# Hymba-style layer on one core: values and gates in 512 columns, two groups' MLP down by Strassen–Winograd with weight sums kept in scratch

## The chip, the cores and the metric

The kernel runs on one core of a Trainium2 chip. The metric is the device time of one execution in microseconds (us). Engines are named as in the profile: PE (TensorE) with its weight loads PEld, DVE (VectorE), ACT (ScalarE), POOL (GpSimd), SP (SyncE, which here only issues DMAs); POOL and ACT also issue DMAs.

## What is computed

One layer for 2,048 prompt tokens and 128 sample tokens (8 streams of 16) of width 1,024, all in float32: an HGRN2 recurrence and a banded attention side by side, the output projection, and a squared-ReLU MLP of width 4,096. Cut to what the change touches:

```python
h = rmsnorm(x, norm1_g)
proj = h @ w_in                      # 1024 -> 4 x 512 (hq, hf, hi, hg) + 3 x 512 (aq, ak, av)
hq, hf, hi, hg, aq, ak, av = jnp.split(proj, SPLITS, axis=-1)
o_h, s_new = hgrn2_scan(hq, 1 - fgate, hi, log(fgate), s0)   # hi: the values
o_h = rmsnorm(o_h, hg_norm_g) * silu(hg)                     # hg: the gates
...
x = x + concat([o_h, o_a]) @ w_out
u = rmsnorm(x, norm2_g) @ w_up                               # 1024 -> 4096
x = x + square(relu(u)) @ w_down                             # 4096 -> 1024
y = rmsnorm(x, final_norm_g)
```

## The kernel before, in words

**Products.** Tokens lie in 17 tiles of 128 (tile 16 is the sample). A float32 operand is held as two arrays, hi (rounded to fp32r, by ACT) and lo (the rest, by DVE). Each product of a pair is three matmuls into one PSUM tile, hi·hi, hi·lo and lo·hi (`mm3`, L337 to L339). Matmuls are written here as 128x256, 128x384 and so on, by the columns that stream.

**Weights.** `W` (L294) loads 128x1024 raw values with one DMA of 512 KB on SP's queue and splits them in two pieces of 128x512 (L303 on ACT, L304 on DVE). A weight of 1024x256 is four pieces. The generator `wseq` hands the weights out in the order of use and makes one ahead; the pool `wsp` holds eight pieces.

**Order.** The program is written as Python generators that `weave` interleaves by cost numbers; a list scheduler then fixes each engine's instruction order. On the chip every engine runs its own list strictly in order and waits on semaphores, so a waiting instruction holds up everything behind it on its engine.

**Stages.** `phase_hgrn` (about 0 to 650 us) projects tokens in six groups of two or three tiles (`hgrn_proj`) while the recurrence of the group before runs. The values (column blocks 4 and 5 of `w_in`) and the gates (blocks 6 and 7) are made with tokens on the PSUM partitions, by `tok`, 256 columns at a time: 24 matmuls of 128x256 per tile and block, then an eviction (ACT for values; ACT, POOL L435 and DVE for gates). `phase_att` runs to about 1380 us. `phase_mlp` then runs three groups of 6, 6 and 5 tiles. The transposed normalised input of a group is two SBUF arrays, `h_hi` and `h_lo`. In the course of group 0 `side` also does the sample's attention and output projection (`sample_mixer`), and makes `h` of group 1 (`prepare`, with `transpose_split` and its L117); that of group 2 is made beside group 1.

**One step of the MLP.** A group takes 16 steps (`fc`), each for 256 of the 4,096 hidden columns. Up: four chunks of 24 matmuls 128x384 (128x320 in the group of 5), each followed by ReLU on ACT (L1138), square on DVE (L1139) and the split into `uh` and `ul` (L1141, L1142). Down: for each tile and each 512 output columns, six matmuls 128x512 into one of four PSUM tiles and an add into `y` on DVE (L1161). The next steps' weights are loaded and split beside it. After the last step each tile is normalised and written out.

## Time and profile before

| What | Value |
|---|---|
| Three timed runs | 2984.89, 2985.36 and 2981.88 us, median 2984.89 us |
| The profiled execution, its own time | 2982.84 us |
| Its span in the trace | 2980.8 us |
| Busy share | PE 97%, DVE 59%, ACT 38%, POOL 10% |
| DMA | 328.17 MB, 110 GB/s over the span |
| Granted clock of PE, mean | 0.99 of full speed (2.4 GHz) |

The profile is of one execution. Its time is 2.05 us below the median of the three runs and 2.04 us above its span. Busy shares are means over stages; the windows among the rows below give them by stage. The three-array form of every product shows as three lines, L337, L338 and L339, of equal counts. The times to landing of DMAs count from the issue.

### The profile page before, as it was taken

To read this page: it belongs to the slowest core of one execution; us is meant where nothing else is said; L and a number is where in the kernel's file an instruction comes from. 1 tells how busy PE (TensorE), PEld (TensorE's weight loads), DVE (VectorE), ACT (ScalarE), POOL (GpSimd) and SP (SyncE) were. 2 spreads that over 40 slices of the span, in tenths; PEclk is the share of its full clock that TensorE was granted. 3 is DMA by queue.
4 is the path that set the end of the run, shared out by engine and by line. 5 is a ranking of instruction groups with operands and counts; after the bars stand their busy time and mean duration, and the time that the engine had idled before them with its cause. 6 is when DMAs were issued, how large, how long until landed. Compare 5 with 4: busy or idle time off the path is not lost.

```text
span 2980.8 us, 47227 instructions
## 1 busy us (share of the span) xinstructions
PE 2899.4 (97%) x18967; PEld 2674.6 (90%) x18967; DVE 1748.5 (59%) x3127; ACT 1117.9 (38%) x2290; POOL 292.5 (10%) x491
## 2 busy tenths in 40 slices
PE   8999999989999999998999999999999999999997
PEld 7989999989888899998888999999999999899997
DVE  6665665765556565665556455565555555555554
ACT  5523433435545455553223223232222223323222
POOL 3311231221010101011000000010000000000000
PEclk9999999999999999999999999999999999999999
DMA  8443423434333434447322322242212123222221
GB/s 275 156 126 100 127 94 95 141 103 139 107 119 106 132 105 137 145 155 268 114 85 89 115 85 91 64 156 64 78 57 71 57 69 126 83 78 71 83 73 64
DMA packets 113125, 328.17 MB, mean 110 GB/s; under 512 B 12613, under 2 KB 36937, under 8 KB 112906
## 3 DMA queue, kind: packets, MB, share of 16 engines
q1 hardware_dynamic: 104570, 299.20, 31.7%
q0 software_dynamic: 6320, 18.62, 1.6%
q10 hardware_dynamic: 2016, 7.34, 0.8%
q8 instruction: 148, 2.42, 0.3%
q14 instruction: 71, 0.58, 0.1%
HBM read 292.61 MB, written 32.51 MB: 109 GB/s over the span
## 4 chain that ended last, share of the span: by engine, by line
PE 71%; DVE 2%; ACT 2%; DMA 1%; issue 1%; POOL 0%; SPq 0%; ACTq 0%; POOLq 0%; DVEq 0%
PE mm L337 21%; PE mm L339 21%; PE mm L338 21%; PE ps_oT L788 3%; PE S L781 2%; PE S L759 2%; PE tx L114 1%; DMA x<-x 1%; ACT junk L100 1%; ACT s L772 0%; PE ps_os L850 0%; DVE y L124 0%; DVE wlo L304 0%; POOL r L92 0%; ACT whi L303 0%
## 5 line engine op out<-in xcount | busy, mean ns | idle before, releaser
L303 ACT CAST whi<-wraw 128x512 fp32r<-128x512 f32 x816 | 498.7, 620 | 723.5 <-PE mm L339 555.1
L304 DVE TENSOR_TENSOR wlo<-wraw,whi 128x512 fp32r<-128x512 f32 x816 | 572.4, 717 | 224.0 <-ACT whi L303 215.9
L337 PE MATMUL mm<-h_hi,whi 128*128 128x384 f32 (+1 forms) x1536 | 504.4, 328 | 3.4 <-DVE h_lo L117 3.4
L339 PE MATMUL mm<-h_hi,wlo 128*128 128x384 f32 (+1 forms) x1536 | 502.7, 327 | 0.0
L338 PE MATMUL mm<-h_lo,whi 128*128 128x384 f32 (+1 forms) x1536 | 501.9, 327 | 0.0
L1161 DVE TENSOR_TENSOR y<-mm,y 128x512 f32<-128x512 f32 x544 | 373.3, 689 | 219.0 <-PE mm L339 217.2
L339 PE MATMUL mm<-whi,ul 128*128 128x512 f32 x1088 | 424.3, 390 | 0.3 <-DVE ul L1142 0.2
L338 PE MATMUL mm<-wlo,uh 128*128 128x512 f32 x1088 | 424.0, 390 | 0.0
L337 PE MATMUL mm<-whi,uh 128*128 128x512 f32 x1088 | 423.5, 389 | 0.5 <-ACT uh L1141 0.5
L337 PE MATMUL mm<-whi,hT_hi 128*128 128x256 f32 x1264 | 376.7, 298 | 21.1 <-ACT whi L303 7.9
L339 PE MATMUL mm<-whi,hT_lo 128*128 128x256 f32 x1264 | 367.6, 291 | 3.1 <-DVE hT_lo L206 1.8
L338 PE MATMUL mm<-wlo,hT_hi 128*128 128x256 f32 x1264 | 364.3, 288 | 0.3 <-DVE wlo L304 0.3
L337 PEld LDWEIGHTS mm<-h_hi,whi 128*128 128x128 f32 x1536 | 289.4, 188 | 8.3 <-DVE h_lo L117 3.6
L338 PEld LDWEIGHTS mm<-h_lo,whi 128*128 128x128 f32 x1536 | 289.4, 188 | 1.2
L339 PEld LDWEIGHTS mm<-h_hi,wlo 128*128 128x128 f32 x1536 | 289.2, 188 | 0.0
L337 PEld LDWEIGHTS mm<-whi,hT_hi 128*128 128x128 f32 x1264 | 245.0, 194 | 33.9 <-ACT whi L303 8.6
L1139 DVE SCALAR_TENSOR_TENSOR u<-mm,u 128x384 f32<-128x384 f32 (+1 forms) x192 | 102.4, 533 | 281.8 <-ACT u L1138 281.8
L337 PE MATMUL mm<-hT_hi,whi 128*128 128x384 f32 (+1 forms) x768 | 260.3, 339 | 4.1 <-ACT qs L965 4.0
L339 PE MATMUL mm<-hT_hi,wlo 128*128 128x384 f32 (+1 forms) x768 | 253.2, 330 | 1.0 <-DVE wlo L304 1.0
L338 PE MATMUL mm<-hT_lo,whi 128*128 128x384 f32 (+1 forms) x768 | 253.4, 330 | 0.0
L339 PEld LDWEIGHTS mm<-whi,hT_lo 128*128 128x128 f32 x1264 | 245.3, 194 | 8.8 <-issue 3.6
L338 PEld LDWEIGHTS mm<-wlo,hT_hi 128*128 128x128 f32 x1264 | 245.6, 194 | 2.0 <-issue 1.0
(200 smaller groups left out, 4024.8 us busy)
## 6 DMA issues: line engine op xcount, KB each, us to landing
wraw<-in_w_in SPq DMA_DIRECT2D x168, 512.0 KB, 4.1
wraw<-in_w_up SPq DMA_DIRECT2D x96, 512.0 KB, 3.9
wraw<-in_w_down SPq DMA_DIRECT2D x96, 512.0 KB, 4.0
wraw<-in_w_out SPq DMA_DIRECT2D x48, 512.0 KB, 3.9
xT<-in_x_T SPq DMA_DIRECT2D x34, 512.0 KB, 3.9
og<-og SPq DMA_DIRECT2D x17, 512.0 KB, 3.8
x<-yo POOLq DMA_DIRECT2D x68, 128.0 KB, 3.3
x<-x SPq DMA_DIRECT2D x17, 512.0 KB, 5.0
```

The source lines that it names most:

```text
L100: nc.scalar.activation(junk[:, :n], x, AF.Square, accum_out=ss)
L114: nc.tensor.transpose(ps[:, k, :], src[:, (k0 + k) * P:(k0 + k + 1) * P], c.ident)
L303: nc.scalar.copy(hi, rw)
L304: nc.vector.tensor_tensor(out=lo, in0=rw, in1=hi.bitcast(F32), op=ALU.subtract)
L337: nc.tensor.matmul(ps, lh, rh, start=(i == 0), stop=False)
L338: nc.tensor.matmul(ps, lh, rl, start=False, stop=False)
L339: nc.tensor.matmul(ps, ll, rh, start=False, stop=(i == n - 1))
L759: nc.tensor.matmul(S[:, bk, :n], a[es, qc], c.K[ft][es, b, kc], start=(a is q and not b), stop=(a is ql))
L781: nc.tensor.transpose(ps[:, x, :], s[:, x * P:(x + 1) * P], c.ident)
L788: nc.tensor.matmul(poT[64 * e:64 * e + 64, j, :], g.vt[i - nk + 1 + x][:, 64 * h:64 * h + 64], pts[e][:, x, :], start=(x == 0), stop=(x == ...
L1139: nc.vector.scalar_tensor_tensor(out=u2, in0=ps, scalar=0.0, in1=u2, op0=ALU.max, op1=ALU.mult)
L1161: nc.vector.tensor_tensor(out=ysl, in0=ps, in1=ysl, op=ALU.add)
```

## The change

**Values and gates.** `tok` takes both blocks at once. A new class `W2` puts two column blocks side by side (four raw rows of K each half), each tile has one PSUM tile of 512 columns, all tiles run the first half of K, then the second, and are evicted 512 columns wide. The PSUM pool of that stage has three tiles instead of two, that of the transposes one instead of two. `wseq` looks ahead by pieces (eight) instead of by one weight.

**Groups.** The MLP's groups have 5, 6 and 6 tiles, so group 0 is now the one of 5.

**Group 0** keeps the plain product. Beside each of its 16 steps a new `Quarters` loads four quarter blocks of `w_down` (128x512, 256 KB, on POOL's queue, L320 of the new kernel), forms four sums of them on POOL (L326), splits four results (L342 on ACT, L343 on DVE) and writes hi and lo of each to scratch `td` with eight DMAs of 256 KB on POOL's queue (L331). The splits go through one buffer `whi` and one `wlo` (pool `m_q`). In all there are 64 loads, 64 sums, 64 splits and 128 DMAs out.

**Groups 1 and 2** take 512 hidden columns a step: two ups of 96 matmuls 128x384 each, and then seven products of three PSUM tiles, six matmuls 128x512 each, where the plain form has eight: 126 matmuls instead of 144. Of the seven weights four come ready split from scratch (`WT`, four DMAs of 256 KB on SP), three are raw and split as before. The seven left operands are four halves of `u` and three combinations, made with four POOL operations 128x768 (`comb`) and seven splits 128x768 (L1346 on ACT, L1347 on DVE). The products are added up in SBUF arrays e0 to e3 (L1388 on DVE; by ACT copies in a group's first step) and recombined after the last step (`sums`, `close`, `leave`, during the next group's first ups). Group 1 has eight such steps, group 2 seven and two plain steps at the end: 15 in all.

**The input of groups 1 and 2** is normalised and transposed ahead, as before, but written to scratch `hd` (`prepare_away`), and read back (`fetch`: 16 DMAs of 128x768, 393 KB each, on SP) into the one `h` pair after the last up of the group before.

Over the whole program the matmuls change in two kinds only: 128x256 from 4464 to 2832 and 128x512 from 3264 to 3810; 128x384 stays at 4992 and 128x320 at 1536.

```diff
-GROUPS_M = [list(range(0, 6)), list(range(6, 12)), list(range(12, 17))]
+GROUPS_M = [list(range(0, 5)), list(range(5, 11)), list(range(11, 17))]
...
+class Quarters:
+    def __init__(self, c, pool, i, k):
...
+                raw = pool.tile([P, PIECE], F32, tag=f"b{a}{b}", name="bq")
+                c.nc.gpsimd.dma_start(out=raw, in_=c.w_down[2 * i + a, b][:, self.ks])
...
+    def sums(self):
+        b = self.b
+        for o, x, y in ((0, 1, 0), (1, 3, 1), (3, 3, 0), (2, 3, 2)):
+            self.c.nc.gpsimd.tensor_tensor(out=b[o], in0=b[x], in1=b[y], op=ALU.subtract)
+
+    def away(self):
+        for n, x in enumerate((0, 3, 1, 2)):
+            for d, y in zip(self.c.td[self.i][n], wsplit(self.c, self.b[x], self.pool)):
+                self.c.nc.gpsimd.dma_start(out=d[:, self.ks], in_=y.bitcast(F32))
+
+def wsplit(c, rw, pool=None):
+    hi = (pool or c.wsp).tile([P, PIECE], F32R, tag="whi", name="whi")
+    lo = (pool or c.wsp).tile([P, PIECE], F32R, tag="wlo", name="wlo")
...
+    nc.scalar.copy(h, rw)
+    nc.vector.tensor_tensor(out=l, in0=rw, in1=h.bitcast(F32), op=ALU.subtract)
...
+class WT(W):
...
+            for x, y in zip((hi, lo), d):
+                c.nc.sync.dma_start(out=x.bitcast(F32), in_=y[:, o:o + PIECE])
...
+            pss = []
+            for half in range(2):
+                w = next(c.ws)
+                for j in range(len(tiles)):
+                    if not half:
...
+                        pss.append(c.ps_mm.tile([P, 512], F32, tag="mm", name="mm"))
...
+                    for k in range(4):
+                        kk = 4 * half + k
+                        hi, lo = hT.hi[:, kk, ts], hT.lo[:, kk, ts]
+                        nc.tensor.matmul(ps, hi, w.hi(k, W512), start=(kk == 0), stop=False)
+                        nc.tensor.matmul(ps, hi, w.lo(k, W512), start=False, stop=False)
+                        nc.tensor.matmul(ps, lo, w.hi(k, W512), start=False, stop=(kk == KT - 1))
...
+def fetch(c, g, hd):
+    h_tiles(c.h0p, g)
+    for k in range(KT):
+        for d, x in zip(hd, (g.hi, g.lo)):
+            c.nc.sync.dma_start(out=x.bitcast(F32)[:, k, :], in_=d.rearrange("p (k n) -> p k n", k=KT)[:, k, :])
...
+                    comb(a[0][0], a[0][0], a[1][0], ALU.subtract)
+                    comb(a[1][0], a[1][0], a[1][1], ALU.add)
+                    ops.append(usplit(a[1][0]))
...
+                    for p in range(7):
+                        w = next(c.ws)
+                        h, l = ops[p]
+                        for j in range(3):
...
+                            list(mm3(c, ps, [(h[:, k, ts], l[:, k, ts], w.hi(k, full), w.lo(k, full))
+                                             for k in range(2)]))
+                            if i:
+                                nc.vector.tensor_tensor(out=acc[p][j], in0=ps, in1=acc[p][j], op=ALU.add)
+                            else:
+                                nc.scalar.copy(acc[p][j], ps)
+                        after(p)
...
+        run(weave(group0(c.h0, GROUPS_M[0], lambda: fetch(c, h1, c.hd[0])), 16.0, side(), 26.0))
+        w = wino([(h1, GROUPS_M[1], lambda: fetch(c, h2, c.hd[1])), (h2, GROUPS_M[2], None)])
+        sp = next(w)
+        run(weave(w, 32.0, prepare_away(c, sp, GROUPS_M[2], c.hd[1]), 16.0))
```

**The order in group 0.** ACT in the third step of group 0, before (L846 belongs to the sample's attention):

```order
L1138 ACTIVATE u2_16267<-mm_16242 128x384 [waits PE_49]
L1141 CAST uh_16240<-u2_16267 128x384 [waits DVE_49]
L846 COPY pn_15815<-tr_16212 128x128 [waits DVE_49]
L1138 ACTIVATE u2_16297<-mm_16272 128x384 [waits PE_49]
L1141 CAST uh_16240<-u2_16297 128x384 [waits DVE_49]
L1138 ACTIVATE u2_16327<-mm_16302 128x384 [waits PE_49,Activation_49]
L303 CAST whi_16374<-wraw_16372 128x512 [waits DMAHW1_49,PE_49]
L1141 CAST uh_16240<-u2_16327 128x384 [waits DVE_49]
L303 CAST whi_16378<-wraw_16372 128x512 [waits PE_49]
L303 CAST whi_16384<-wraw_16382 128x512 [waits DMAHW2_49,PE_49]
L303 CAST whi_16388<-wraw_16382 128x512 [waits PE_49]
```

and in the third step of group 0 now, where L1259 is the ReLU, L1297 the split of `u`, `wraw` a weight of the product and `bq` a quarter or a sum of quarters that goes to scratch; the number behind `bq` is its buffer:

```order
L1259 ACTIVATE u2_15466<-mm_15441 128x320 [waits PE_49]
L1297 CAST uh_15434<-u2_15466 128x320 [waits DVE_49]
L342 CAST whi_16308<-bq_16054 128x512 [waits DMASW3_49,Activation_49,Pool_49]
L1259 ACTIVATE u2_15496<-mm_15471 128x320 [waits PE_49]
L342 CAST whi_15537<-wraw_15535 128x512 [waits DMAHW6_49,PE_49]
L1297 CAST uh_15434<-u2_15496 128x320 [waits DVE_49]
L342 CAST whi_15541<-wraw_15535 128x512 [waits PE_49]
L342 CAST whi_15547<-wraw_15545 128x512 [waits DMAHW7_49,PE_49]
L342 CAST whi_16314<-bq_16060 128x512 [waits DMASW6_49,Activation_49,Pool_49]
L1259 ACTIVATE u2_15526<-mm_15501 128x320 [waits PE_49]
L342 CAST whi_15551<-wraw_15545 128x512
L1297 CAST uh_15434<-u2_15526 128x320 [waits DVE_49]
```

Splits of sums now stand among the ReLUs, in ACT's one list. The first of the 64 stands just ahead of the first ReLU of group 0, and all 64 stand ahead of the second ReLU of the ninth step of the 16. Between those two ReLUs' matmuls PE's list has 792 matmuls 128x320, 480 of 128x512, 240 of 128x256 and 72 small ones.

POOL at that place before has only the sample's small operations:

```order
L822 COPY kT_16825<-ksam_15803 128x4x16 [waits DMAHW0_49,PE_49]
L836 MEMSET pz_16802 128x128 [waits PE_49]
L822 COPY kT_17122<-ksam_15803 128x4x16 [waits DMAHW4_49,PE_49]
L836 MEMSET pz_16841 128x128 [waits PE_49]
L836 MEMSET pz_17138 128x128 [waits PE_49]
L90 TENSOR_SCALAR r_17444<-ss_17442 128x1 [waits Activation_49]
L92 TENSOR_TENSOR r_17444<-r_17444,mhalf_71 128x1 [waits Pool_49]
L731 DMA og_73<-oa_17439 128x512 [waits DVE_49]
```

Now, where t13lo is the last piece of one step of sums, and t20 to t23 are the next:

```order
L331 DMA t13lo_97<-wlo_15971 128x512 [waits DMASW4_49,DVE_49]
L320 DMA bq_16058<-in_w_down 128x512 [waits DMASW5_49]
L326 TENSOR_TENSOR bq_16054<-bq_16056,bq_16054 128x512 [waits DMASW2_49]
L326 TENSOR_TENSOR bq_16056<-bq_16060,bq_16056 128x512 [waits DMASW7_49,Pool_49]
L326 TENSOR_TENSOR bq_16060<-bq_16060,bq_16054 128x512 [waits Pool_49]
L331 DMA t20hi_98<-whi_16308 128x512 [waits DMASW6_49,Activation_49]
L326 TENSOR_TENSOR bq_16058<-bq_16060,bq_16058 128x512 [waits DMASW5_49,Pool_49]
L331 DMA t20lo_99<-wlo_16309 128x512 [waits DVE_49]
L320 DMA bq_16387<-in_w_down 128x512 [waits DMASW0_49]
L331 DMA t21hi_100<-whi_16314 128x512 [waits DMASW1_49,Activation_49]
L331 DMA t21lo_101<-wlo_16315 128x512 [waits DVE_49]
```

The loads of the next quarters, the four sums and the eight DMAs out of a step of sums stand in one list, and a DMA out waits for ACT or DVE, a sum for the load.

**The order at the end of group 1.** SP before has only weight loads there:

```order
L298 DMA wraw_24450<-in_w_down 128x1024 [waits DMAHW0_49,DVE_49]
L298 DMA wraw_24582<-in_w_down 128x1024 [waits DMAHW1_49,DVE_49]
L298 DMA wraw_24592<-in_w_up 128x1024 [waits DMAHW2_49,DVE_49]
L298 DMA wraw_24602<-in_w_up 128x1024 [waits DMAHW3_49,DVE_49,Activation_49]
L298 DMA wraw_24708<-in_w_down 128x1024 [waits DMAHW4_49,DVE_49]
L298 DMA wraw_24840<-in_w_down 128x1024 [waits DMAHW5_49,DVE_49]
L298 DMA wraw_24850<-in_w_up 128x1024 [waits DMAHW6_49,DVE_49]
```

Now the 16 DMAs of `fetch` stand between the scratch weight of the third product (t70) and that of the fourth (t73); the 10 rows of `fetch` between these two pieces are like those shown:

```order
L357 DMA whi_24359<-t70hi_138 128x512 [waits DMAHW3_49,PE_49]
L357 DMA wlo_24360<-t70lo_139 128x512 [waits PE_49]
L357 DMA whi_24363<-t70hi_138 128x512 [waits DMASW2_49,PE_49]
L357 DMA wlo_24364<-t70lo_139 128x512 [waits DMASW3_49,PE_49]
L1230 DMA h_lo_24336<-hd1lo_81 128x768 [waits PE_49]
L1230 DMA h_hi_24335<-hd1hi_80 128x768 [waits PE_49]
L1230 DMA h_hi_24335<-hd1hi_80 128x768 [waits DMAHW1_49]
```

and behind them:

```order
L1230 DMA h_lo_24336<-hd1lo_81 128x768 [waits DMAHW4_49]
L1230 DMA h_hi_24335<-hd1hi_80 128x768 [waits DMAHW5_49]
L1230 DMA h_lo_24336<-hd1lo_81 128x768 [waits DMAHW6_49]
L357 DMA whi_24367<-t73hi_144 128x512 [waits DMAHW7_49]
L357 DMA wlo_24368<-t73lo_145 128x512 [waits DMAHW0_49,DMASW7_49]
L357 DMA whi_24371<-t73hi_144 128x512 [waits DMAHW1_49,DMASW3_49]
L357 DMA wlo_24372<-t73lo_145 128x512 [waits DMAHW2_49,DMASW4_49]
```

The `fetch` stands ahead of the last four products' weights of that step.

**The order in a Strassen step.** DVE before, at the start of a down:

```order
L304 TENSOR_TENSOR wlo_23015<-wraw_23008,whi_23014 128x512 [waits PE_49,Activation_49]
L1139 SCALAR_TENSOR_TENSOR u2_22983<-mm_22958,u2_22983 128x384 [waits Activation_49]
L1161 TENSOR_TENSOR y_20843<-mm_23018,y_20843 128x512 [waits PE_49]
L1142 TENSOR_TENSOR ul_22867<-u2_22983,uh_22866 128x384 [waits Activation_49]
L1161 TENSOR_TENSOR y_20843<-mm_23026,y_20843 128x512 [waits PE_49]
L1161 TENSOR_TENSOR y_20845<-mm_23034,y_20845 128x512 [waits PE_49]
L1161 TENSOR_TENSOR y_20845<-mm_23042,y_20845 128x512 [waits PE_49]
```

DVE now, at the start of a step's products (e0, e2 and e1 are the sums of products; a is `u`; ul the lo part of a left operand):

```order
L1347 TENSOR_TENSOR ul_22124<-a_21887,uh_22123 128x768 [waits Activation_49]
L1260 SCALAR_TENSOR_TENSOR a_21889<-mm_22127,a_21889 128x384 [waits Activation_49]
L1388 TENSOR_TENSOR e0_20175<-mm_22176,e0_20175 128x512 [waits PE_49]
L1347 TENSOR_TENSOR ul_22157<-a_21888,uh_22156 128x768 [waits Activation_49]
L1388 TENSOR_TENSOR e0_20176<-mm_22184,e0_20176 128x512 [waits PE_49]
L1388 TENSOR_TENSOR e0_20177<-mm_22192,e0_20177 128x512 [waits PE_49]
L1347 TENSOR_TENSOR ul_22201<-a_21889,uh_22200 128x768 [waits Activation_49]
L1388 TENSOR_TENSOR e2_20181<-mm_22212,e2_20181 128x512 [waits PE_49]
L1347 TENSOR_TENSOR ul_22237<-a_21886,uh_22236 128x768 [waits Activation_49]
L1388 TENSOR_TENSOR e2_20182<-mm_22220,e2_20182 128x512 [waits PE_49]
L1388 TENSOR_TENSOR e2_20183<-mm_22228,e2_20183 128x512 [waits PE_49]
L1347 TENSOR_TENSOR ul_22274<-a_21889,uh_22273 128x768 [waits Activation_49]
```

Between the evictions stand the splits of operands that POOL has made.

## Rows read from the trace of the kernel before

**Rows 1.** The page: span, busy time of each engine, granted clock by slice.

```profile
span 2980.8 us, 47227 instructions
PE 2899.4 (97%) x18967; PEld 2674.6 (90%) x18967; DVE 1748.5 (59%) x3127; ACT 1117.9 (38%) x2290; POOL 292.5 (10%) x491
PEclk9999999999999999999999999999999999999999
```

**Rows 2.** Windows: us, PE, PEld, DVE, ACT, POOL busy, PEclk, DMA share, GB/s.

```profile
0.00:600.00 600.00, 567.68 (x4304) 546.99 (x4305) 394.82 (x779) 257.89 (x575) 151.23 (x246) 0.99 0.44 139
1380.00:1980.00 600.00, 593.84 (x3237) 540.26 (x3238) 328.42 (x571) 175.01 (x333) 20.16 (x50) 0.99 0.32 104
2000.00:2200.00 200.00, 200.00 (x1026) 182.58 (x1025) 110.69 (x177) 56.93 (x106) 1.48 (x4) 1.00 0.24 77
```

**Rows 3.** Timeline of PE, 128x256, first and last of 24 in a row.

```profile
300.03 0.28 PE L337 MATMUL mm<-whi,hT_hi 128*128 128x256 f32 x1
...
302.79 0.28 PE L339 MATMUL mm<-whi,hT_lo 128*128 128x256 f32 x1
```

**Rows 4.** Timeline of PE: first and last of 24 at 128x384, of 72 at 128x512.

```profile
2199.74 0.33 PE L337 MATMUL mm<-h_hi,whi 128*128 128x384 f32 x1
...
2203.72 0.33 PE L339 MATMUL mm<-h_hi,wlo 128*128 128x384 f32 x1
2203.90 0.39 PE L337 MATMUL mm<-whi,uh 128*128 128x512 f32 x1
...
2220.03 0.39 PE L339 MATMUL mm<-whi,ul 128*128 128x512 f32 x1
```

**Rows 5.** Timeline of ACT: the first ReLU of three steps of group 0.

```profile
1389.18 0.49 ACT L1138 ACTIVATE u<-mm 128x384 f32<-128x384 f32 x1 [6.87 <-PE mm L339]
...
1426.29 0.47 ACT L1138 ACTIVATE u<-mm 128x384 f32<-128x384 f32 x1
...
1465.30 0.47 ACT L1138 ACTIVATE u<-mm 128x384 f32<-128x384 f32 x1
```

**Rows 6.** Groups by form: count, busy us, mean ns, idle before and its releasers.

```profile
L304 DVE TENSOR_TENSOR wlo<-wraw,whi 128x512 fp32r<-128x512 f32 x816 | 572.4, 717 | 224.0 <-ACT whi L303 215.9 <-PE mm L338 4.1 <-PE S L759 0.4
L303 ACT CAST whi<-wraw 128x512 fp32r<-128x512 f32 x816 | 498.7, 620 | 723.5 <-PE mm L339 555.1 <-PE mm L338 92.2 <-DMA wraw<-in_w_in 24.1
L1161 DVE TENSOR_TENSOR y<-mm,y 128x512 f32<-128x512 f32 x544 | 373.3, 689 | 219.0 <-PE mm L339 217.2
```

**Rows 7.** POOL operations of two sizes: duration in ns, min/median/max.

```profile
L435 POOL TENSOR_TENSOR sig<-sig,hgain x34: 722/743/1531, 81.3 to 599.5; 128x256 f32<-128x256 f32 x34
L193 POOL TENSOR_TENSOR xT<-xT,g x31: 1887/1897/2544, 25.1 to 1160.8; 128x1024 f32<-128x1024 f32 x31
```

**Rows 8.** 256 KB DMAs issued by POOL at L731: issue (ns), landing (us).

```profile
L731 POOL DMA_DIRECT2D og<-bias x16: 539/608/608, 771.4 to 1333.3; - x16
...
DMA to landing us min/median/max: 2.4/3.3/6.0
```

**Rows 9.** Windows with the densest DMA traffic; the last column is GB/s.

```profile
1390.00:1394.00 4.00, 4.00 (x25) 4.00 (x24) 0.96 (x3) 1.00 (x2) 0.00 (x0) 1.00 1.03 420
1402.00:1406.00 4.00, 4.00 (x19) 3.31 (x18) 3.83 (x8) 1.02 (x3) 1.40 (x3) 1.00 1.05 387
```

**Rows 10.** Durations of DVE's L206 in ns, min/median/max.

```profile
L206 DVE TENSOR_TENSOR hT_lo<-xT,hT_hi x31: 1212/1226/2502, 97.0 to 1220.3; 128x1024 fp32r<-128x1024 f32 x31
```

**Rows 11.** Timeline of POOL and DVE around 103 us: start, duration.

```profile
102.53 1.90 POOL L193 TENSOR_TENSOR xT<-xT,g 128x1024 f32<-128x1024 f32 x1
...
103.00 2.50 DVE L206 TENSOR_TENSOR hT_lo<-xT,hT_hi 128x1024 fp32r<-128x1024 f32 x1
```

**Rows 12.** PE after a pause, and the window behind it (columns as in Rows 2).

```profile
75.61 0.47 PE L542 MATMUL ps_sc<-qp,ks 128*128 128x64 f32 x1 [4.29 <-DVE sc L525]
76.00:78.00 2.00, 2.00 (x11) 2.00 (x11) 0.54 (x2) 0.00 (x0) 0.00 (x0) 0.50 0.83 303
```

**Rows 13.** Waits: who waited for whom, us in total, times, longest.

```profile
PE mm L337 <- DVE h_lo L117: 9.4, 3, 3.4
```

More of the change, by code (lines that the diff above doesn't have):

```diff
@@ L324, in wseq @@
     yield None
-    for x in srcs[1:]:
-        nxt = W(c, *x)
+    while ahead:
+        n, w = ahead.pop(0)
+        used -= n
+        fill(n)
         yield w
-        w = nxt
-    yield w
 def mm3(c, ps, pairs, parts=1):
@@ new lines, in phase_mlp, with pool @@
+    HALF = GMAX // 2
+    full = slice(0, 512)
+    top = ExitStack()
+    base = top.enter_context(ExitStack())
+    def pool(s, name, bufs, **k):
+        return s.enter_context(tc.tile_pool(reuse_waits="tile", name=name, bufs=bufs, **k))
+    cp = pool(base, "m_const", 1)
+    c.ps_mm = pool(base, "m_psmm", 4, space=PSUM)
+    c.ps_tx, c.ps_tx_tag = pool(base, "m_pstx", 2, space=PSUM), "tx"
+    c.ps_smp = pool(base, "m_pssmp", 2, space=PSUM)
+    c.g2 = gain_tile(c, cp, "g2", c.norm2_g)
+    gf = gain_tile(c, cp, "gf", c.final_g)
@@ new lines, in plain @@
+    def plain(g, tiles, ys, dst, usplit, at, then=None):
+        n = len(tiles) * P
+        up(next(c.ws), g, n, dst, usplit)
+        if then:
+            then()
+        wd = next(c.ws)
+        for j, y in enumerate(ys()):
+            for dc, w in enumerate(wd):
+                ps = c.ps_mm.tile([P, 512], F32, tag="mm", name="mm")
+                list(mm3(c, ps, [at(k, j) + (w.hi(k, full), w.lo(k, full)) for k in range(2)]))
+                ysl = y[:, dc * 512:(dc + 1) * 512]
+                nc.vector.tensor_tensor(out=ysl, in0=ps, in1=ysl, op=ALU.add)
+            yield j
@@ new lines, in group0, with dst, usplit, at @@
+    def group0(g, tiles, nxt):
+        with ExitStack() as s:
+            pu = pool(s, "m_u", 1)
+            pu2 = pool(s, "m_u2", 2)
+            pq = pool(s, "m_q", 1)
+            py = pool(s, "m_y", len(tiles))
+            st = {}
+            ys = []
+            def dst(f, cs):
+                if not f and not cs.start:
+                    st["h"], st["l"] = (pu.tile([P, 2, GMAX], F32R, tag=x, name=x) for x in ("uh", "ul"))
+                return pu2.tile([P, 384], F32, tag="u2", name="u2")[:, :cs.stop - cs.start]
+            def usplit(f, cs, u):
+                h = st["h"][:, f, cs]
+                nc.scalar.copy(h, u)
+                nc.vector.tensor_tensor(out=st["l"][:, f, cs], in0=u, in1=h.bitcast(F32), op=ALU.subtract)
+            def at(k, j):
+                ts = slice(j * P, (j + 1) * P)
+                return st["h"][:, k, ts], st["l"][:, k, ts]
+            def get():
+                if not ys:
@@ L1166, in mlp @@
[L1166 to L1181 removed]
+                return ys
```

359 lines of the change are left out of this document (244 added, 115 removed).

## The prediction

> **What bounds the kernel now.** I read the page first: PE is busy for 2899.4 of the span's 2980.8 us, at full granted clock in every slice [rows 1]. No other engine is near that: DVE has 59%. Then the windows, since a share over the span hides the stages: PE is busy for 568 of 600 us in the recurrence's stage, 594 of 600 in group 0 of the MLP, and 200 of 200 in group 1 [rows 2]. So each matmul taken away in the MLP brings its spacing, as long as no other engine's work, made dearer or later, comes to stand in front of PE. The timeline of PE gives the spacings: 23 intervals of 128x256 in 2.76 us are 0.120 us each [rows 3], 23 of 128x384 in 3.98 us 0.173, and 71 of 128x512 in 16.13 us 0.227 [rows 4]. Doubling 256 columns costs less than double.
>
> **Values and gates.** 1632 matmuls 128x256 become 816 of 128x512: 1632 × 0.120 = 195.8 against 816 × 0.227 = 185.2, so −10.6 us. The evictions keep their elements. PE idles 32 us in this stage for the recurrence's sake [rows 2], and one PSUM tile more and one less can shift that by some microseconds to either side; I count zero, with −8 and +8 as ends.
>
> By the Trainium skill (TensorE: Matmul & The Clock Gate, section Back-to-back issue gap) the isolated gap of two matmuls is N/2.4 + 2.5 ns, which is 109 ns for 256 columns and 216 for 512: by it this part would bring 2 us instead of 11. The trace's 120 ns at 256 columns disagrees, and the trace decides [rows 3].
>
> **Strassen's products.** 15 steps with 126 matmuls in place of 144 are 270 fewer: 270 × 0.227 = −61.3 us. Moving the group of five tiles to the front changes no count. All this is on PE's path, because groups 1 and 2 have no idle PE [rows 2].
>
> **Group 0's chain of sums.** This is the term that decides. All 64 splits stand in ACT's list ahead of the second ReLU of the ninth step, so ACT, and PE with it, gets there only when the chain through one `whi` and one `wlo` has got there. How long does PE need that far? 792 matmuls 128x320 at 0.1465 (between the 256 and 384 of rows 3 and 4) are 116 us, 480 × 0.227 = 109, 240 × 0.120 = 29, together 254. For the 72 small ones: steps of group 0 take 37.1 and 39.0 us [rows 5], where their plain matmuls give 96 × 0.173 + 72 × 0.227 = 33.0, so the sample's work in a step is 4.0 to 6.0, in eight steps 32 to 48; 29 of that is counted already. That leaves 3 to 19, and 257 to 273 in all; four PSUM tiles let PE run another 5 us ahead. I take 272, which is 17.0 us for each of the 16 fours of splits.
>
> What does the chain need? A split's subtraction of 0.72 [rows 6] must wait until the DMA before it has landed, since there is one `wlo`. A DMA of this size issued by POOL takes 0.6 to issue and lands 2.4 to 6.0 us after the start of its issue, 3.3 at the median [rows 8]. With 0.1 for the handing over, three of four splits take 4.1 each (3.2 at the shortest landing). For the first of each four, POOL's list has between two DMAs of lo: that DMA and a load (0.6 each), three sums, a DMA (0.6) and the fourth sum. A sum of 512 columns lies between 0.74 and 1.90 for 256 and 1024 columns [rows 7], linearly 1.13; 1.8 + 4 × 1.13 = 6.3, and 7.4 if DVE holds two sums up by half a microsecond each (below). Four splits take 6.3 + 3 × 4.1 = 18.6 to 19.7, at the shortest landing 15.9. I take 19.2. The chain is then 2.2 late per four, and 16 × 2.2 = +35 us stand on PE's path. The ends are 0 (landing at 2.5) and +75 (landing at 4.1, period 21.7). DVE has room for it: 328 busy of 600 us before [rows 2], and 64 × 0.72 = 46 more; ACT and POOL have more. I do not go below zero, since the chain adds work and takes none away.
>
> **Fetch at a group's end.** 6.3 MB at the 387 to 420 GB/s of the densest windows [rows 9] are 15 to 16 us. At the end of group 1 SP's list has the fetch ahead of the fourth product's weight, so that weight lands some 21 us after the last up, with the first three products (54 × 0.227 = 12.2 us) to cover it: 8 to 10 us idle. After an idle time of 4.3 us the granted clock was half at 76 to 78 us [rows 12], so some half-clock matmuls come on top. I take +11, ends 4 and 16. At the end of group 0 the down of 60 matmuls (13.6 us) and a plain step's weights, already there, cover it: +1, ends 0 and 6.
>
> **A Strassen step on DVE and POOL.** In 126 × 0.227 = 28.6 us of products DVE has 21 evictions at 0.69, six splits of raw weights at 0.72 [rows 6] and five of the operands' splits at 0.97 (768 columns, between the 0.72 for 512 and 1.23 for 1024 of rows 6 and 10): 14.5 + 4.3 + 4.9 = 23.7. It fits, if POOL does not stop it. POOL's four combinations of 768 columns at 1.5 [rows 7] are 6 us. Four PSUM tiles hold 5.4 us of matmuls, which covers a single late eviction. I take 0.7 us a step, +10 for 15; ends 0 and 30.
>
> **The seams.** At the end, DVE's adds for the output stand behind 15 POOL adds of 1.1 ahead of a square that PE's next chunk needs: +4, ends 0 and 9. At the start PE waited up to 3.4 us for the last tile of `h` [rows 13]; with five tiles instead of six that is due earlier: −3, ends −6 and 0.
>
> **Sum.** −10.6 − 61.3 + 35 + 12 + 10 + 4 − 3 = −13.9 us. The profiled execution's own time is 2982.84, so 2968.9; it lies 2.05 below the median of the three runs, 2984.89, so a median of 2971.0.
>
> **Rivals.** *The chain keeps up.* Landings of 2.4 to 2.8 give 15.9 to 17.1 per four, the chain costs 2 at most, and with the other terms between their low ends and their values the time is 2911 to 2938. For it: the shortest landings of rows 8. Against: their median.
>
> *The chain sets the pace.* The 128 DMAs out and 64 loads are 50 MB, in 272 us 185 GB/s, on top of the 104 of that stage [rows 2]: 289, of some 400 at the densest [rows 9]. Queues behind weight loads then lengthen landings. From 20.4 us per four (a landing of 3.5 to 3.9) the whole change is slower by over 6 us; at 4.1 to 4.9 the period is 21.0 to 23.4, the chain costs 64 to 102, and the time is 3000 to 3038. For it: landings up to 6.0 in a stage with less traffic [rows 8].
>
> *DVE and POOL shut each other out.* An L206 that began while POOL's L193 ran took 2.50 us instead of 1.23 [rows 10, 11]: POOL ended at 104.43, DVE 1.07 later, so it did nearly all of its work after POOL. If every combination stops DVE for its 1.5 us, a step's DVE time is 23.7 + 6.0 = 29.7 of 28.6, and DVE is the bound by 1.1 us; with late evictions at each start, 15 steps cost 18 to 30 instead of 10. With the longer sums in group 0 (19.7 per four, +43) the time is 2987 to 2999, or 2979 to 2991 where the chain stays as forecast. The Trainium skill (SBUF — State Buffer, section Who interferes with whom) says that a DVE instruction with two SBUF inputs and a GpSimd instruction that reads SBUF exclude each other for the whole instruction; the trace agrees, 2.50 us against 1.23. It speaks against this change, whose sums and combinations are all such. Evictions have one input in PSUM, and the trace of before has none beside POOL, so how many are stopped stays open.
>
> **Chances.** Forecast (2945 to 2979) 0.36; the chain keeps up (under 2945) 0.18; shut out, near no change (2979 to 2991) 0.16; slower (over 2991: chain or both) 0.30. A measurement here tells about 0.2%, 6 us, from no change, so faster 0.54, same 0.16, slower 0.30. Range: 2926 to 3032, leaving out the upper part of the slow case and the best of the fast; the forecast's own is 2945 to 2979.
>
> **What would show it.** In the trace of after: 24 matmuls of 128x512 in the values' stage at 0.227, and PE not idle there for more than some 32 us. In group 0 the starts of L343 on `bq` four by four: 17 us or less, 18 to 20, or over 20.4; PE's waits there for ACT's ReLU or `uh`, with the ReLU itself ready behind an L342 that waits for a DMA. At the end of group 1 an idle PE of 8 to 10 us behind the third product, ended by a scratch weight's DMA. In a Strassen step 21 evictions in 28.6 us, and whether L1347 takes 0.97 or up to 2.5. The prediction is wrong if landings are far from 3.3, if PE waits in every Strassen step, or if PE waits for something not named here, such as the scratch weights on SP.

## The result, and the profile after

The changed kernel takes 3056.35 us at the median (3054.52 to 3060.13) against 2985.12 of the kernel before in the same comparison: 1.0238 times as long, with an interval of 1.0223 to 1.0253. It is slower by 71 us, where 2971 had been forecast and 3032 was the end of the range. The profiled execution has a span of 3053.0 us, 72.2 more than before.

The page of the changed kernel, the same rows as [rows 1]:

```profile
span 3053.0 us, 46272 instructions
PE 2879.8 (94%) x17881; PEld 2610.9 (86%) x17881; DVE 1800.6 (59%) x3056; ACT 1165.5 (38%) x2313; POOL 647.9 (21%) x820
PEclk9999999999999999998898999999999999999998
```

PE has 1086 matmuls fewer, but its busy time fell by only 20 us, and its clock is down in the slices around 1400 to 1700 us and in the last. The windows by stage say where (us, PE, PEld, DVE, ACT, POOL busy, PEclk, DMA share, GB/s; compare [rows 2]):

```profile
1387.00:1773.00 386.00, 314.59 (x1702) 276.79 (x1701) 225.35 (x379) 120.34 (x245) 201.55 (x287) 0.87 0.67 220
1773.00:2011.00 238.00, 237.94 (x1368) 218.01 (x1367) 142.51 (x232) 83.28 (x162) 12.17 (x23) 1.00 0.45 145
2465.00:2535.00 70.00, 57.77 (x277) 50.91 (x275) 40.00 (x45) 14.88 (x25) 30.26 (x20) 0.92 0.53 188
2926.00:3053.00 127.00, 101.58 (x488) 89.44 (x487) 80.04 (x98) 30.54 (x50) 34.61 (x30) 0.91 0.30 100
```

The first is group 0 while its chain of splits runs, the second group 0 without it: PE idles 71 us in the one, nothing in the other. The third is the seam of groups 1 and 2, the fourth the end. What PE waited for, in its timeline (the idle time before, and its releaser, in brackets):

```profile
1402.71 0.79 PE L431 MATMUL mm<-whi,uh 128*128 128x512 f32 x1 [9.87 <-ACT uh L1297]
1432.93 0.47 PE L942 MATMUL tr<-ident,pz 128*128 128x128 f32 x1 [8.65 <-DVE pz L936]
2495.03 0.77 PE L431 MATMUL mm<-whi,uh 128*128 128x512 f32 x1 [8.52 <-DMA whi<-t73hi]
2987.38 0.80 PE L431 MATMUL mm<-whi,uh 128*128 128x512 f32 x1 [11.60 <-ACT uh L1346]
```

Two of these are named in the prediction, t73 at the seam and the chain's hold on `uh`; the DVE rows `pz`, of the sample's attention, are held in the same way, behind splits in DVE's list. ReLUs give the pitch: the first and the 33rd of group 0, and of group 1 the first two of one step, in one row, and the second of each of the two steps behind it:

```profile
1386.90 0.43 ACT L1259 ACTIVATE u<-mm 128x320 f32<-128x320 f32 x1
1773.09 0.43 ACT L1259 ACTIVATE u<-mm 128x320 f32<-128x320 f32 x1
...
2011.25 0.87 ACT L1259 ACTIVATE a<-mm 128x384 f32<-128x384 f32 x2 [1.19 <-PE mm L433]
2073.50 0.49 ACT L1259 ACTIVATE a<-mm 128x384 f32<-128x384 f32 x1 [2.29 <-PE mm L433]
2136.28 0.49 ACT L1259 ACTIVATE a<-mm 128x384 f32<-128x384 f32 x1 [2.25 <-PE mm L433]
```

Eight steps of group 0 took 386.2 us. A Strassen step takes 62.8 us in the middle of group 1, where two plain steps are 192 × 0.173 + 144 × 0.227 = 65.9 [rows 4]: it does what it was made for.

### The profile page after: what moved, and what is told of

Same layout as the page of the kernel before. It is cut to its first block, busy times and chain, and to the rows that moved or that the text cites. A ratio compares the mean times of both kernels' runs of the same rounds, so it can differ in the third digit from the quotient of the medians.

```text
span 3053.0 us, 46272 instructions
## 1 busy us (share of the span) xinstructions
PE 2879.8 (94%) x17881; PEld 2610.9 (86%) x17881; DVE 1800.6 (59%) x3056; ACT 1165.5 (38%) x2313; POOL 647.9 (21%) x820
## 3 DMA queue, kind: packets, MB, share of 16 engines
q8 instruction: 140, 2.29, 0.3%
## 4 chain that ended last, share of the span: by engine, by line
PE 40%; DMA 5%; POOL 3%; DVE 3%; issue 3%; ACT 1%; SPq 0%; POOLq 0%; DVEq 0%; ACTq 0%
PE mm L431 13%; PE mm L433 13%; PE mm L432 13%; DVE wlo L343 1%; POOL bq L326 1%; POOL e L1397 1%; DMA bq<-in_w_down 1%; PE ps_os L949 0%; DMA wraw<-in_w_up 0%; PE tx L1215 0%; DMA t62lo<-wlo 0%; ACT whi L342 0%; ACT junk L100 0%; DMA x<-x 0%; POOL bq L320 0%
## 5 line engine op out<-in xcount | busy, mean ns | idle before, releaser
L343 DVE TENSOR_TENSOR wlo<-wraw,whi 128x512 fp32r<-128x512 f32 x786 | 557.4, 727 | 225.2 <-ACT whi L342 221.3
L342 ACT CAST whi<-wraw 128x512 fp32r<-128x512 f32 x786 | 474.5, 619 | 452.3 <-PE mm L433 227.9
L433 PE MATMUL mm<-whi,ul 128*128 128x512 f32 x998 | 394.0, 395 | 2.5 <-DVE ul L1298 2.5
L432 PE MATMUL mm<-wlo,uh 128*128 128x512 f32 x998 | 393.9, 395 | 0.0
L431 PEld LDWEIGHTS mm<-whi,uh 128*128 128x128 f32 x998 | 190.6, 191 | 99.4 <-ACT uh L1297 24.8
L1363 POOL TENSOR_TENSOR a<-a 128x768 f32<-128x768 f32 x60 | 120.3, 2005 | 666.0 <-DVE a L1260 594.3
L90 POOL TENSOR_SCALAR r<-ss 128x1 f32<-128x1 f32 (+1 forms) x85 | 29.2, 343 | 974.6 <-ACT junk L100 745.2
L1260 DVE SCALAR_TENSOR_TENSOR a<-mm,a 128x384 f32<-128x384 f32 x128 | 71.0, 556 | 275.8 <-ACT a L1259 275.8
L433 PEld LDWEIGHTS mm<-whi,ul 128*128 128x128 f32 x998 | 190.1, 190 | 44.8 <-DVE ul L1298 4.1
L431 PE MATMUL mm<-whi,hT_hi 128*128 128x256 f32 x720 | 215.6, 299 | 8.6 <-DVE h_lo L117 7.2
L432 PEld LDWEIGHTS mm<-wlo,uh 128*128 128x128 f32 x998 | 190.3, 191 | 38.8 <-DMA wlo<-t73lo 0.3
L433 PE MATMUL mm<-whi,hT_lo 128*128 128x256 f32 x720 | 209.3, 291 | 1.0 <-DVE hT_lo L117 1.0
```

The costliest lines, as they stand in the source:

```text
L90: nc.gpsimd.tensor_scalar(out=r[:, :n], in0=ss, scalar1=1.0 / width, scalar2=EPS, op0=ALU.mult, op1=ALU.add)
L342: nc.scalar.copy(h, rw)
L343: nc.vector.tensor_tensor(out=l, in0=rw, in1=h.bitcast(F32), op=ALU.subtract)
L431: nc.tensor.matmul(ps, lh, rh, start=(i == 0), stop=False)
L432: nc.tensor.matmul(ps, lh, rl, start=False, stop=False)
L433: nc.tensor.matmul(ps, ll, rh, start=False, stop=(i == n - 1))
```

## The experiments

Theory at the start: the chain of sums, splits and DMAs in group 0, bunched by the order into eight steps and led through one buffer, set PE's pace there. Rivals: the traffic of its 50 MB; POOL's sums holding DVE up; the Strassen steps and seams themselves. In the table "33 ReLUs" is the time from the first to the 33rd ReLU of group 0, and "a four" is the mean time of four splits (from the first to the last of the 64 starts of L343 or its counterpart, 4/63 of it), both from the timelines.

| Kernel | Median, us | Ratio to before | 33 ReLUs, us | A four, us |
|---|---|---|---|---|
| changed kernel | 3056.35 | 1.0223 to 1.0253 | 386 | 24.7 |
| e0 no chain | 2972.33 | 0.9934 to 0.9965 | 285 | none |
| e1 two buffers | 3051.39 | 1.0191 to 1.0236 | 384 | 19.9 |
| e2 chain in two steps only | 2970.51 | 0.9921 to 0.9966 | 307 | none after |
| e3 no sums | 3014.84, one run | | 351 | 22.0 |
| e4 small DMAs out | 3035.49, one run | | 369 | 22.4 |
| e5 paced | 2984.14 | 0.9983 to 1.0018 | 298 | 33.6 |
| e9 two buffers, same places | 3021.75 | 1.0096 to 1.0142 | 357 | 20.9 |

**e2: the chain in two steps only.**

```diff
-                q = Quarters(c, pq, fc // 2, fc % 2)
+                q = Quarters(c, pq, 0, fc) if fc < 2 else None
-                        srcs.append((2, lambda i=i, x=x: WT(c, c.td[i][x])))
+                        srcs.append((2, lambda i=i, x=x: WT(c, c.td[0][x])))
```

> The changed kernel, with the sums, splits and DMAs to scratch made in the first two steps of group 0 only; all 15 Strassen steps read that first set from scratch, so the weights of 14 of them are not theirs and the output is not the reference's. All reads and matmuls stay. Theory (the chain in group 0 is what made the change slower): 14 of 16 fours go, the time falls by some 14/16 of 116 us, 100, to 2945 to 2970, below the kernel before. Rival (the Strassen steps, the fetch or the values' stage lose it): the time falls by less than 50 us and stays above 3005.

The time fell by 86 us, just short of what was written and far from the rival's side: the loss lies in the chain. The two steps that kept it took 46 and 37 us, the others without heavy work of the sample 30 to 34.

**e0: no chain at all.** The scratch is filled by eight copies from `w_down` at the start of the MLP instead.

> The changed kernel with no load, sum, split or DMA of quarters in group 0 at all; the scratch weights that all Strassen steps read are filled once, at the start of the MLP, with eight copies of raw weights (so the weights are not the right ones and the output is not the reference's). Theory (the chain costs what e2's remaining two steps and the paced e5 point to): the first 33 ReLUs in 280 to 300 us instead of 386, the time 2945 to 2965, that is 90 to 110 us for the chain, where the prediction had 35. Rival (part of the 386 us is the sample's work, wherever the chain stands): 300 to 320 us, the time 2965 to 2980.

```profile
1404.67 0.44 ACT L1259 ACTIVATE u<-mm 128x320 f32<-128x320 f32 x1 [4.75 <-PE mm L433]
...
1690.13 0.43 ACT L1259 ACTIVATE u<-mm 128x320 f32<-128x320 f32 x1
```

In its ACT timeline the 33 ReLUs take 285.5 us, as the theory had it: the chain costs 386.2 − 285.5 = 100.7 us. The time itself missed what was written and lies where the rival put it, by the means of the experiment: the eight copies put the first ReLU off from 1386.90 to 1404.67. Less these 17.8 us it would be 2954.6, an estimate.

**e5: the same work, paced.** The split's copy gets a factor 1.0 that is made from one chunk of an up, so that the order has one split per chunk, over 16 steps.

```diff
+                if "q" in st:
+                    one = c.small.tile([P, 1], F32, tag="one", name="one")
+                    nc.vector.tensor_scalar(out=one, in0=u[:, 0:1], scalar1=0.0, scalar2=1.0, op0=ALU.mult, op1=ALU.add)
+                    st["q"].away(st["n"], one[:, 0:1])
...
+        nc.scalar.activation(h, rw, AF.Copy, scale=one)
```

> The changed kernel, with one split of a weight sum per chunk of an up, spread over all 16 steps of group 0 (the split's factor 1.0 is made from that chunk's result, so the order cannot draw it ahead); one buffer as before. The same work in all. Theory (the order draws 16 fours of splits into eight steps, and one four needs 24 us of the 17 that PE has there, while a step has some 33): group 0's stall goes nearly whole, the time falls by 80 to 110 us to 2945 to 2975. If instead single splits ahead of ReLUs hold PE up wherever they stand (rival C): the time falls by less than 50 us and stays above 3005.

```profile
1381.01 0.44 ACT L1261 ACTIVATE u<-mm 128x320 f32<-128x320 f32 x1 [2.54 <-PE mm L435]
...
1679.15 0.43 ACT L1261 ACTIVATE u<-mm 128x320 f32<-128x320 f32 x1
```

The 33 ReLUs take 298.1 us: 88 of the 100.7 go, with every load, sum, split and DMA still there. So for the most part it is neither their work nor their bytes, but where they stand. The time fell by 72 us, not 80 to 110, since the last four splits now stand behind the last up: group 0's last step took 46 us instead of 33, and the others behind the 33rd ReLU, which now have splits too, 13 us more together.

**e1 and e9: two buffers.**

```diff
+    kw = dict(bufs=2) if pool is not None else {}
-    hi = (pool or c.wsp).tile([P, PIECE], F32R, tag="whi", name="whi")
-    lo = (pool or c.wsp).tile([P, PIECE], F32R, tag="wlo", name="wlo")
+    hi = (pool or c.wsp).tile([P, PIECE], F32R, tag="whi", name="whi", **kw)
+    lo = (pool or c.wsp).tile([P, PIECE], F32R, tag="wlo", name="wlo", **kw)
```

> The changed kernel, with two buffers instead of one for the hi and the lo of the weight sums that group 0 splits; nothing else. In the changed kernel the time from the first ReLU of group 0 to the 33rd is 386 us, where PE has some 270 us of work, and a four of splits takes 24.3 us. Theory (the one buffer makes each split wait for the DMA before it to land, and the splits stand in the lists of ACT and DVE ahead of what PE waits for): a four falls to 12 to 18 us, the stretch to 275 to 310 us, the time by 60 to 110 us to 2945 to 2995. Rival A (the traffic of the 50 MB, not the waiting for one buffer, makes it slow) and rival B (POOL's sums hold DVE up): a four stays over 21 us and the time over 3020.

A miss. A four became faster, 19.9 instead of 24.7 us, but the scheduler used the second buffer to draw the 64 splits further ahead, ahead of the 29th ReLU, where the last stood behind the 33rd, and the 33 ReLUs took as long. In e9 the splits are tied to the places that they have in the changed kernel, two per chunk:

> The changed kernel, with two buffers for hi and lo as in e1, and with the splits tied to the chunks of group 0's ups at two per chunk, so that they stand where they stand in the changed kernel (all 64 ahead of the 33rd ReLU) instead of further ahead as in e1. Theory (e1 gained nothing since its order drew the splits ahead of the 28th ReLU, and a four still took 19.5 us against the 15 to 17 that PE has there; both the buffer and the bunching cost): a four at 18 to 21 us, the first 33 ReLUs in 310 to 350 us instead of 386, the time 3010 to 3030. Rival (the one buffer costs nothing; it is the queues of POOL and DVE): still 375 to 390 us, the time over 3045.

At these places the second buffer is worth 29 us of the 33 ReLUs (357 against 386), less than written. The bunching is the larger part: spreading the splits takes away 88 us with one buffer (386 to 298 in e5) and 51 with two (357 to 306 in e14, below).

**e4 and e3: the bytes and the sums.**

```diff
-                self.c.nc.gpsimd.dma_start(out=d[:, self.ks], in_=y.bitcast(F32))
+                n = 64 if self.i else PIECE
+                self.c.nc.gpsimd.dma_start(out=d[:, self.ks.start:self.ks.start + n], in_=y.bitcast(F32)[:, :n])
```

> The changed kernel, where the DMAs to scratch write 64 of the 512 columns, except for the first set, which every Strassen step reads (the weights of 14 steps are not theirs, and the output is not the reference's). Same number of DMAs, 29 MB fewer bytes. Theory (each split waits for a fixed time until a DMA has landed): a four stays at 20 us or more, the time falls by at most 30 us. Rival A (traffic): a four falls below 18 us and the time by 70 us or more, below 2990.

112 of the 128 DMAs write an eighth, which is 26 MB fewer bytes; the 29 written there count all 128. They take 17 us from the 33 ReLUs: traffic has a share, a small one. For e3 the call `q.sums()` is left out:

> The changed kernel without POOL's 64 sums in group 0 (the quarters are split and sent to scratch as loaded, so the Strassen weights are not the right ones and the output is not the reference's); loads, splits and DMAs stay. Theory (the chain's first link of each four is POOL's own list, with four sums of 1.3 us): a four falls by 4 to 6 us from 24.7 to 19 to 21, the first 33 ReLUs come in 315 to 350 us, the time falls by 40 to 75 us to 2980 to 3015. Rival (landings and the lists of ACT and DVE alone set it): a four falls by less than 2 us, the time by less than 20.

35 us, with a four at 22.0: a gain of 2.7 us per four where 4 to 6 was written; the time, 3014.84, is at the slow end of what was written. From copy to copy the link that has the sums falls only from 7.6 to 6.2 us, and the other three, 6.2, 6.0 and 4.9 before, are 5.4, 5.2 and 5.1. Without the sums the first link waits for landings as the others do, so taking some 5 us of sums out brings little: the links do not simply add up.

**e7: values and gates alone.** The kernel before, with `W2`, the new `tok` and `wseq`'s look-ahead.

> The kernel before, with only the values' and gates' part of the change: 512 columns at a time, the three PSUM tiles, and the weights made ahead by pieces; MLP as before. Theory (the part was costed rightly at -10.6 us, as far as the recurrence's stage ends 8.3 us earlier in the changed kernel): 7 to 11 us faster than the kernel before. Rival (the gain is taken back by later waits, since the first ReLU of the MLP came only 2.3 us earlier): within 4 us of the kernel before.

2977.80 us against 2987.20, ratio 0.9953 to 0.9978: 9.4 us faster. As forecast, by the medians. The profiled execution is the slowest of twelve, 2983.04, and does not show it: its first ReLU comes at 1391.16, where it came at 1389.18 before.

**e6 and e10: the fetch.**

```diff
-            c.nc.sync.dma_start(out=x.bitcast(F32)[:, k, :], in_=d.rearrange("p (k n) -> p k n", k=KT)[:, k, :])
+        c.nc.scalar.dma_start(out=x.bitcast(F32), in_=d.rearrange("p (k n) -> p k n", k=KT))
```

> The changed kernel, with each fetch as two DMAs of 3.1 MB on ACT's queue instead of 16 on SP's, so that the scratch weights of a step's last four products no longer stand behind them. In the changed kernel PE stood 8.5 us behind the third product at the end of group 1, until t73 landed, and the stretch from the first ReLU of group 1's last step to that of group 2 took 85.3 us, where an undisturbed step takes 62.8. Theory (SP's order makes the weight late): the 8.5 us go to under 3, the stretch falls by 8 to 15 us, the time by as much, to 3041 to 3049. Rival (the 6.3 MB themselves fill the DMA engines, whichever queue they are on): the wait stays over 6 us, the time within 4 us of the changed kernel.

3066.75 us, ratio 1.0244 to 1.0290: no gain, but 10 us more than the changed kernel. ACT's timeline at the end of group 1 shows a new wait in the place of the old:

```profile
2487.02 0.35 ACTq L1229 DMA_DIRECT2D h_lo<-hd1lo  x1
2487.42 0.49 ACT L1258 ACTIVATE a<-mm 128x384 f32<-128x384 f32 x1 [2.43 <-PE mm L433]
2501.97 0.33 ACTq L1229 DMA_DIRECT2D h_hi<-hd1hi  x1
2502.34 2.30 ACT L1345 CAST uh<-a 128x768 fp32r<-128x768 f32 x3 [14.43 <-DMA wlo<-t72lo]
```

The second DMA's issue waited 15 us, by the trace until a scratch weight on SP's queue (t72lo) had landed, and the splits of operands stood behind it in ACT's list. PE also waited 7.4 us at the start of group 1, for `h_hi`, where the changed kernel has no such wait. So the same with POOL's queue (`gpsimd` for `scalar`):

> The changed kernel, with each fetch as two DMAs of 3.1 MB on POOL's queue, where no earlier DMA's landing is waited for, as the second one on ACT's queue did in e6 (issued 15 us after the first, with the splits of operands behind it). Theory (SP's order made t73 late): no wait of PE over 4 us behind the third product, the stretch from group 1's last first ReLU to group 2's falls from 85.3 to 70 to 77, the time falls by 8 to 15 us to 3041 to 3049. Rival (the 6.3 MB fill the DMA engines): the wait stays over 6 us, the time within 4 us of the changed kernel.

Rows of e10: PE in the timeline, the fetch in the source view, and the DMAs of one scratch weight, t72lo, beside the fetch:

```profile
2499.66 0.79 PE L432 MATMUL mm<-wlo,uh 128*128 128x512 f32 x1 [5.08 <-DMA wlo<-t73lo]
```

```profile
DMA to landing us min/median/max: 13.8/17.8/21.4
```

```profile
DMA to landing us min/median/max: 19.0/19.3/19.6
```

The wait is 5.1 instead of 8.5 us, between what theory and rival had written. The stretch across the seam is 82.3 instead of 85.3 (from the second ReLU of group 1's last step to that of group 2's first, in both runs), the time 3066.38 (1.0244 to 1.0282), 10 us more than the changed kernel, where the rival had written within 4. Its profiled execution, 3057.10, is the fastest of four. At the start of group 1 PE waits 8.8 us for `h_hi`, so the fetch loses there what it gains here; the rest of the 10 us is not explained. So the order of SP's queue gives some 3 us of the wait at most, and the traffic the rest: beside the fetch six DMAs of scratch weights landed 17.7 to 19.6 us after their issue, though the fetch was on another queue; elsewhere in this run they took 2.4 to 7.2 us.

**e11 and e15: the end.** In e11 the DVE adds of the last recombination were written behind the chunks of the up:

```diff
-                later.extend([[S[0]], [S[1], C[0]], [S[2], C[1]], [C[2]]])
+                later.extend([[S[0]], [S[1]], [S[2]], [C[0]]])
```

> The changed kernel, with the last recombination's DVE adds behind the four chunks of the plain step's up, one third of them ahead of its down and the others between its evictions, instead of between the chunks. In the changed kernel PE stood 11.6 us there: DVE waited 7.6 us for POOL's adds, and then had adds of 128x1024 ahead of the squares. Theory: the 11.6 us fall to under 4, the time falls by 7 to 13 us to 3043 to 3050. Rival (the adds have to be done anyway before the down can be evicted, so the wait only moves): the time within 4 us of the changed kernel.

3057.31 us, and DVE's rows stood in the order of the changed kernel: the scheduler drew the adds ahead again, and the run tells nothing about the theory. In e15 they are tied to the last chunk's square by a factor 1.0, as in e5:

> The changed kernel with only the end of e14: the DVE adds of the last recombination are made to depend on the last chunk's square, so that the order has them behind the chunks. Theory (DVE's list made PE wait 11.4 us): the wait falls under 4 us, the time by 6 to 13 us to 3043 to 3051. Rival (the adds and POOL's sums have to be done anyway): the time within 4 us of the changed kernel.

```profile
2980.62 0.80 PE L431 MATMUL mm<-whi,uh 128*128 128x512 f32 x1 [2.43 <-DVE e L1278]
```

PE's longest wait there is 2.4 us instead of 11.6, and the time 3045.11 (1.0180 to 1.0212), 11 us less. The list made PE wait, not the work.

**e12 and e14: put together.**

> The splits paced one per chunk as in e5, with the fetch on POOL's queue and the late adds of e11. If each takes away its own wait: the 2984 of e5 less 8 to 15 for the fetch and 7 to 13 for the end, 2956 to 2969, 18 to 31 us below the kernel before. If one of the two only moves its wait: 2969 to 2977. If neither helps: 2980 to 2988.

2985.34 us (0.9989 to 1.0007), as e5 and as written for the case that neither helps: its end is that of e11, which was none, and its fetch on POOL's queue had the up at the start of group 1 wait 8.0 us for `h_lo`. The fetch is back on SP in e14, with two buffers, one split per chunk from the first chunk on, and the end of e15:

> One split per chunk from the first chunk on, so that the last set ends with the last up (in e5 four splits came behind it, and its last step took 46 us instead of 33), with two buffers, and the last recombination's DVE adds tied behind the fourth chunk's square (in e11 the scheduler had left the order as it was). If the rest of the chain's price in e5 was its tail and the one buffer, and the end's wait comes from the order: group 0 in 530 to 545 us instead of 562, the end 7 to 13 us less, the time 2940 to 2965, 20 to 45 us below the kernel before. If pacing leaves a price of single waits in every step: 2965 to 2985.

2972.18 us, ratio 0.9937 to 0.9962: 13.6 us faster than the kernel before and 84 faster than the changed one. Group 0 took 555 us, where 530 to 545 was written: the 33 ReLUs take 306 us against 285 in e0, with five short waits of PE of 1.3 to 3.8 us, four of them for DVE. Pacing leaves a price.

## Why the prediction was wrong

**Group 0's chain: the step that failed.** It was the right term ("the term that decides") with the wrong size, +35 where e0 gives +101. The rival called "the chain sets the pace" had that right, but for another reason: it wanted landings of 4.1 to 4.9 us, and they were no longer than forecast (below). PE's need was sized nearly rightly: 272 us against 285 in e0. The chain's was not: 18.6 to 19.7 us a four against 24.7. The 64 splits of the changed kernel's timelines give the links. From one copy to the next it was 7.6 us from the last of a four to the first of the next, and then 6.2, 6.0 and 4.9, where the prediction had 6.3 to 7.4 once and 4.1 three times. So the first link was nearly right and the other three, the mere waits for a landing, were short by 1.6 us each on average. ACT's copies of one four (start, duration, and the wait before):

```profile
1498.24 0.61 ACT L342 CAST whi<-bq 128x512 fp32r<-128x512 f32 x1
...
1504.77 0.62 ACT L342 CAST whi<-bq 128x512 fp32r<-128x512 f32 x1 [4.04 <-DMA t21hi<-whi]
...
1508.75 0.62 ACT L342 CAST whi<-bq 128x512 fp32r<-128x512 f32 x1 [3.36 <-DMA t22hi<-whi]
```

POOL's list at that place:

```profile
1497.60 0.56 POOL L331 DMA_DIRECT2D t20lo<-wlo  x1
1498.15 0.55 POOL L320 DMA_DIRECT2D bq<-in_w_down  x1
1499.15 0.54 POOL L331 DMA_DIRECT2D t21hi<-whi  x1 [0.44 <-ACT whi L342]
1501.12 0.54 POOL L331 DMA_DIRECT2D t21lo<-wlo  x1 [1.44 <-DVE wlo L343]
1501.65 0.55 POOL L320 DMA_DIRECT2D bq<-in_w_down  x1
1505.68 0.54 POOL L331 DMA_DIRECT2D t22hi<-whi  x1 [3.48 <-ACT whi L342]
```

The landing itself was sized well enough. The source view of the DMAs out says

```profile
DMA to landing us min/median/max: 2.3/2.7/7.0
```

so the median was even better than the 3.3 of [rows 8], and the mean of the 128 is 3.3. The Trainium skill (DMA: Bandwidth & Descriptors, section Anatomy of one DMA — SWDGE (gpsimd) path) fits 2.0 us + bytes/436,000, which gives 2.6 us for 256 KB, an estimate; the trace's median of 2.7 agrees with that. What was left out stands around the landing. I counted only lo's loop (a subtraction, a DMA, a landing). But hi has a loop of its own, copy, issue, landing, copy, and lo's subtraction needs both: it began 2.6 to 3.3 us after its copy's end in these three positions. From an issue for hi to the next copy it was 3.3 to 4.9 us there on average; t21hi, issued at 1499.15 right behind two other transfers of POOL's queue, let the next copy start 5.6 us later.

And the chain's parts stand in the lists among the step's own work, which the sum left out too. Of the 63 subtractions behind the first, 30 began when lo's DMA had landed, 4 when their copy was done, and 29 only when the instruction ahead of them in DVE's list was done, 2.3 us after all that they needed themselves was there (mean). Those ahead were squares, whose ReLU stood behind a copy for the chain in ACT's list, and adds and outputs that waited for PE.

Seen from PE the 101 us look like this. In e0's window

```profile
1404.67:1690.13 285.46, 281.39 (x1732) 255.50 (x1731) 161.82 (x309) 88.90 (x181) 11.84 (x30) 0.99 0.35 117
```

PE is idle for 4 us and busy for 281; in the changed kernel's it is idle for 71, where the chain held `uh` or `pz`, and busy for 315, at a granted clock of 0.87 instead of 0.99. So some 67 us are waits and some 33 a lower clock. I had reckoned with half clock at the seam, and not here. This is the same loss as that of the links, not one more beside it; whether slower matmuls lengthened the links in turn was not tried.

**Values and gates:** −10.6 forecast, −9.4 measured in e7 (6.6 to 14.0 by its interval). Right.

**Strassen's products and the steps:** The products' −61.3 was right, and the +10 for DVE and POOL nearly all too much. The pitch is 62.8 us in group 1 and 61.9 in group 2, where the full gain is 192 × 0.173 + 126 × 0.227 = 61.8. The 0.9 of group 1 are eight transposes a step, for the input of group 2, and no price of the change: a plain step of group 1 took 33.9 us with them and 33.0 without, before. So a step costs 0.1 us where 0.7 was forecast. L1347 shows the hold-up by POOL, in 28 of its 120 operations, all beside an operation of POOL:

```profile
L1347 DVE TENSOR_TENSOR ul<-a,uh x109: 943/959/2292, 2024.5 to 3024.8; 128x768 fp32r<-128x768 f32 x109
```

The evictions, of which the prediction left it open, were not held up:

```profile
L1388 DVE TENSOR_TENSOR e<-mm,e x273: 673/683/694, 2099.8 to 2969.5; 128x512 f32<-128x512 f32 x137
```

62 of them ran beside an operation of POOL of over 1 us, and none of these took more than 692 ns. (The trace of before had a few as well, against what the prediction says of it: five of L1161, at 682 to 684 ns.)

**The seam:** PE's wait for t73 was forecast at 8 to 10 us, and is 8.52. From the second ReLU of group 1's last step to that of group 2 it is 85.3 us, though, some 23 over the 62.0 of a step without transposes, where I had 11: behind the wait come 3.3 and 3.9 us for squares that stand in DVE's list among the recombination's work, and matmuls at a granted clock of 0.92. And the cause was half right: e10 gives the queue's order 3 us of the 8.5 and the traffic the rest.

**The end:** +4 forecast; e15 gains 11 by moving it. The mechanism was right (DVE waits for POOL ahead of squares); that DVE's own adds of 128x1024, three of them doubled in length beside POOL, come on top of the wait was not in the sum:

```profile
2967.33 2.29 DVE L1397 TENSOR_TENSOR e<-e,e 128x1024 f32<-128x1024 f32 x1 [7.60 <-POOL e L1397]
...
2977.39 1.21 DVE L1397 TENSOR_TENSOR e<-e,e 128x1024 f32<-128x1024 f32 x1
```

**The start:** −3 was not seen. The recurrence's last output came 8.3 us earlier than before (651.1 against 659.4), the first ReLU only 2.3 (1386.90 against 1389.18 [rows 5]). The windows between the two, before and after:

```profile
659.37:1389.18 729.81, 709.39 (x5806) 648.19 (x5807) 429.33 (x800) 371.67 (x774) 87.14 (x139) 0.99 0.43 136
651.14:1386.90 735.76, 717.41 (x5834) 656.19 (x5835) 423.56 (x797) 369.57 (x771) 89.50 (x141) 0.98 0.42 138
```

PE waits no longer, but is busy for 8 us more at a lower clock, 0.980 against 0.988. That is scatter of single executions and not the change: the runs with the changed kernel's code in this stage took 724.9 (e12) to 735.8 us for it.

Together, for the two profiled executions: −2.3 at the first ReLU, −61.3 with some +1 for the steps, +101, some +23 for the seam and the first step behind it, +11: +72, of 72.2 seen. That it fits to the us is luck, by the scatter of that stage.
